# Later modulation columns: multiplied and summed by VectorE, only summed over partitions by TensorE

## The chip, the cores and the metric

The kernel runs on one core of a Trainium2 chip. The metric is device time in microseconds (us) of one launch, the median of several runs. Engines are named as the profile names them: PE (TensorE), DVE (VectorE), ACT (ScalarE), POOL (GpSimd), SP (SyncE, which issues the DMAs here).

## The reference

Two layers of a mixer over 512 latent and 256 context tokens, width 1024, fp32. What matters here is the modulation and where it is used:

```
mod   = silu(c) @ w_mod + b_mod            # 1024 -> 3 x 1024, per layer
mod_c = silu(c_ctx) @ w_mod + b_mod        # the same map for the context tokens
shift, scale, gate = split(mod, 3)
h = rmsnorm(x, norm_w) * (1 + scale) + shift
... three branches from h @ w_in: attention, SSD (Mamba-2), convolution ...
y = g0 * (ua @ w_br_attn) + g1 * (us @ w_br_ssd) + g2 * (uc @ w_br_conv)   # g: sigmoid gates of h
x_new = x + gate * (y @ w_out)             # the last layer keeps only the latent tokens
```

So for each layer 24 blocks of 128 columns (8 shift, 8 scale, 8 gate) are products of a 1024 x 128 weight block with two vectors, silu(c) and silu(c_ctx). Shift and scale are needed at the start of a layer, the gate only in its output projection.

## The kernel before

Activations lie with channels on the 128 partitions and tokens along the row. A projection of 1024 channels is 8 channel tiles deep; each fp32 weight tile is split into a high and a low part (whi by ACT, L156; wlo by DVE, L157), and three products (hi x hi, hi x lo, lo x hi) are summed in one PSUM bank. `wload` (L140) loads a weight tile into one of three `raw` buffers and splits it into five half-tile buffers, at a raised priority (TOP).

The kernel is written in Tile, whose scheduler fixes each engine's order ahead of the run, by priority (program order, less a bonus where the code raises it). From the `man` block (L475) to the end of the attention (L1118) PE's order is as written. There the merges of branch 2 (convolution) and branch 1 (SSD) are woven as small steps between the steps of the SSD scan and of the attention by `Weave` (L190), which paces them by columns (`merge_cols`, L744). The last merge (branch 0, attention; `merge_steps(0, ..., fin=True)`, L1129) and the output projection (`out_tile`, L1147) come after it, and there the scheduler chooses PE's order too.

A merge goes over 8 channel tiles `ct`. Each has a gate (`sig_steps`, 24 products per span of tokens, evacuated by ACT with a tanh) unless that gate is ready in DRAM (`ready`), and the branch product (12 products per span), which DVE evacuates and multiplies with the gate (`br_out`, L718). Both use the PSUM pool `pj`, which has two banks. Layer 0 has spans of 512 and 256 tokens, layer 1 one of 512. In layer 0's last merge tiles 1, 3 and 5 have their gates ready, in layer 1's 1, 3, 5 and 7.

The modulation columns of layer 0 that its start needs (shift and scale, 16 blocks) are made by `mod_tiles` (L221) and don't change. The others, 8 blocks of layer 0 and 24 of layer 1, are made in groups of four blocks, and each group in two halves, `mod_half` (L244): two loads of 512 KB, then 16 matmuls in which a 128 x 32 piece of `sc` (silu(c) and silu(c_ctx) in columns 0 and 1, the rest zero) is the stationary operand and a 128 x 128 weight block moves, on four column groups of PE side by side. ACT copies the first half out of PSUM, DVE adds the second (L262), PE transposes the sum (L266), and DVE adds the bias (L267). One half is a visit. Layer 0's four visits stand in the loop over the convolution projections of the SSD branch (L549); layer 1's twelve stand in layer 0's three merges, one after every second channel tile (L738), and the transposition is put off by MOD_LAG columns of other work (`then`, L674).

Of the kernel before, what the change touches and what calls it, by code (L numbers as in the profile page):

```python
# [15 lines left out]
P = 128  # L16
DM = 1024
KD = DM // P
# [32 lines left out]
MOD_LAG = 12288  # L51
# [6 lines left out]
def hybrid_kernel(ctx, tc, xT, cc, consts, rope, mod_params, params, fnw, w_mod, w_cm, w_q, w_kvd, w_z,  # L58
# [71 lines left out]
    V.memset(nhalf, -0.5)  # L130

# [112 lines left out]
    def mod_half(li, mod, m0, half, part):  # L244


        raws = []
        for i in range(2):
            raw = wp.tile([P, 4, 2, P], F32, tag="raw", name="raw")
            k0 = 4 * half + 2 * i  # L250
            with tc.high_priority(offset=TOP):
                nc.sync.dma_start(raw, w_mod[li, m0:m0 + 4, :, k0:k0 + 2, :].rearrange("m p k c -> p m k c"))
            raws.append(raw)
        ps = pot("ps_mod")
        for i in range(4):
            for j in range(4):
                T.matmul(ps[32 * j:32 * j + 32, 0:P], sc[:, 4 * half + i, :], raws[i // 2][:, j, i % 2, :],
                         start=(i == 0), stop=(i == 3), tile_position=(0, 32 * j))
        if half == 0:
            S.activation(part, ps[:, 0:P], AF.Copy)  # L260
            return None
        V.tensor_tensor(out=part, in0=ps[:, 0:P], in1=part, op=ALU.add)  # L262

        def finish():
            pt = ps[:, P:2 * P]
            T.transpose(pt, part, ident)  # L266
            V.tensor_tensor(  # L267
                out=mod[:, m0:m0 + 4, :], in0=pt.rearrange("p (j r) -> p j r", j=4)[:, :, 0:2],
                in1=pmod[:, li, O_BMOD + m0:O_BMOD + m0 + 4].unsqueeze(2).to_broadcast([P, 4, 2]), op=ALU.add)

        return finish

    class Mods:


        def __init__(self, li, mod, m0):
            self.li, self.mod, self.m0, self.n = li, mod, m0, 0

        def visit(self):
            g, half = divmod(self.n, 2)  # L280
            if half == 0:
                self.part = sm.tile([P, P], F32, tag="part", name="part4")
            self.n += 1
            return mod_half(self.li, self.mod, self.m0 + 4 * g, half, self.part)
# [65 lines left out]
    for li in range(2):  # L350
# [127 lines left out]
        na = sm.tile([P, 16], F32, tag="na", name="na")  # L478
        S.activation(na, par[:, O_AL:O_AL + 16], AF.Exp)
# [52 lines left out]
        gate_mods = Mods(0, mods[0], 16)  # L532
        for ct in range(8):
# [15 lines left out]
            if li == 0 and ct % 2 == 1:  # L549
                fn = gate_mods.visit()  # L550
                if fn is not None:
                    soon.append(fn)
# [121 lines left out]
        def then(fn, steps):  # L674

            done = 0
            for n in steps:
                yield n
                done += n
                if done >= MOD_LAG and fn is not None:  # L680
                    fn()
                    fn = None
            if fn is not None:
                fn()
# [14 lines left out]
        def merge_steps(br, u, first, fin, ready=()):  # L699
# [4 lines left out]
            end = None  # L704
            next_mods = Mods(1, mods[1], 8 * (2, 1, 0)[br])
            for ct in range(KD):
# [15 lines left out]
                if ct in ready:  # L722
                    nc.sync.dma_start(tg, g_dr[ct][:, :ntok])
                else:
                    yield from then(end, sig_steps(br, ct, tg))
                    end = None
                yield from then(end, mm_cm_steps(wb, lambda k: u[0][:, k, :], lambda k: u[1][:, k, :], ntok, br_out,
# [13 lines left out]
            if end is not None:  # L741
                end()
# [556 lines left out]
```

## Time and profile before

| | |
|---|---|
| median of 3 runs | 1493.41 us (1489.54 to 1495.44) |
| the profiled execution | 1494.89 us |
| its span | 1493.1 us |
| mean granted clock of PE | 0.992 of full speed |
| DVE busy | 1037.0 us, 69% |
| ACT busy | 716.4 us, 48% |
| chain that ended last | PE 91%, DVE 2%, ACT 2%, DMA 2% |

A chain's share is the time in which the last instruction's chain of predecessors stood on that engine. An engine's busy time is the union of its instructions; matmuls overlap, so the distance from one start to the next tells more than a matmul's duration. Layer 0's last merge lies from 739 to 812 us, its output stage to 880, layer 1's last merge from 1380 to 1430.

### The profile page before, as it was taken

The numbers are of one execution on the slowest core, as the hardware profiler recorded it, in microseconds if no ns is written. First come the engines' busy times: TensorE is split into PE (matmuls) and PEld (weight loads), VectorE is DVE, ScalarE is ACT, GpSimd is POOL, SyncE is SP. The second block draws the span as 40 slices with busy tenths as digits, with TensorE's granted clock in tenths as the row PEclk, the third lists the DMA queues.
The fourth block names the chain that finished last, engine by engine and source line by source line (L and its number), as shares of the span: only waits on it lengthen the run. The fifth ranks groups of instructions, "written<-read, shape, count | busy, mean of one in ns | idle before, by whom it ended". The sixth has DMA issues, their size and how long they took to land.

```text
span 1493.1 us, 24893 instructions
## 1 busy us (share of the span) xinstructions
PE 1443.5 (97%) x9660; PEld 1252.6 (84%) x9660; DVE 1037.0 (69%) x1895; ACT 716.4 (48%) x1600; POOL 81.7 (5%) x177
## 2 busy tenths in 40 slices
PE   5999999999998999999999999999999999999997
PEld 5889899988887888888888877989988887888886
DVE  4689998665657775555444378999977788666554
ACT  4423543365444476555422254355455547666431
POOL 0000010100001210000000000001010121000000
PEclk9999999999999999999999999999999999999999
DMA  9222343212334323313653532223423342223542
GB/s 376 68 75 94 98 129 111 75 61 99 100 113 135 116 76 129 107 64 121 236 167 105 173 113 87 82 59 114 154 71 108 99 151 80 98 85 99 176 139 81
DMA packets 81975, 172.58 MB, mean 116 GB/s; under 512 B 7872, under 2 KB 40768, under 8 KB 81856
## 3 DMA queue, kind: packets, MB, share of 16 engines
q1 hardware_dynamic: 81856, 170.98, 35.2%
q8 instruction: 76, 1.25, 0.4%
q14 instruction: 43, 0.35, 0.1%
HBM read 143.43 MB, written 27.53 MB: 114 GB/s over the span
## 4 chain that ended last, share of the span: by engine, by line
PE 91%; DVE 2%; ACT 2%; DMA 2%; issue 1%; SPq 0%; POOL 0%; POOLq 0%; DVEq 0%; ACTq 0%
PE ps_gm L175 22%; PE ps_br L175 11%; PE ps_xbc L175 8%; PE ps_o L175 7%; PE ps_gcv L175 4%; PE ps_g L175 4%; PE ps_u L175 3%; PE po_v L1079 3%; PE ps_ga L175 3%; PE pt_p L1065 3%; PE ps_l L1019 2%; PE ps_z L216 1%; PE ps_c L1019 1%; PE ps_q L217 1%; PE ps_q L216 1%; PE ps_z L217 1%
## 5 line engine op out<-in xcount | busy, mean ns | idle before, releaser
L156 ACT ACTIVATE whi<-raw 128x512 fp32r<-128x512 f32 (+1 forms) x316 | 198.9, 632 | 294.7 <-PE ps_gm L175 60.9
L157 DVE TENSOR_TENSOR wlo<-raw,whi 128x512 fp32r<-128x512 f32 (+1 forms) x316 | 216.8, 690 | 150.6 <-ACT whi L156 146.3
L441 DVE SCALAR_TENSOR_TENSOR vacc<-vt,par,vacc 128x783 f32<-128x783 f32 (+1 forms) x232 | 207.0, 892 | 7.9 <-ACT vacc L438 4.2
L175 PE MATMUL ps_gm<-hh,whi 128*128 128x512 f32 (+1 forms) x576 | 212.3, 369 | 0.0
L175 PE MATMUL ps_gm<-hh,wlo 128*128 128x512 f32 (+1 forms) x576 | 209.6, 364 | 0.0
L175 PE MATMUL ps_gm<-hl,whi 128*128 128x512 f32 (+1 forms) x576 | 209.3, 363 | 0.0
L175 PEld LDWEIGHTS ps_gm<-hh,wlo 128*128 128x128 f32 x576 | 109.0, 189 | 15.6 <-issue 2.1
L175 PEld LDWEIGHTS ps_gm<-hh,whi 128*128 128x128 f32 x576 | 109.2, 190 | 15.1 <-issue 2.0
L175 PEld LDWEIGHTS ps_gm<-hl,whi 128*128 128x128 f32 x576 | 109.0, 189 | 14.2 <-issue 1.0
L175 PE MATMUL ps_xbc<-hh,whi 128*128 128x512 f32 (+1 forms) x240 | 82.9, 345 | 0.0
L175 PE MATMUL ps_xbc<-hh,wlo 128*128 128x512 f32 (+1 forms) x240 | 82.1, 342 | 0.0
L175 PE MATMUL ps_xbc<-hl,whi 128*128 128x512 f32 (+1 forms) x240 | 82.0, 342 | 0.0
L175 PE MATMUL ps_o<-yh,whi 128*128 128x256 f32 (+1 forms) x208 | 65.8, 317 | 3.1 <-DVE xnew L1142 3.0
L689 ACT ACTIVATE tg<-ps_gm,hw 128x512 f32<-128x512 f32 x72 | 44.3, 615 | 49.2 <-PE ps_gm L175 48.8
L1071 ACT ACTIVATE pth<-pt_p 128x512 f32<-128x512 f32 x72 | 43.6, 605 | 49.4 <-PE pt_p L1065 49.3
L175 PE MATMUL ps_o<-yl,whi 128*128 128x256 f32 (+1 forms) x208 | 65.7, 316 | 0.0
L175 PE MATMUL ps_o<-yh,wlo 128*128 128x256 f32 (+1 forms) x208 | 65.6, 315 | 0.0
L558 DVE SCALAR_TENSOR_TENSOR xacc<-xraw,par,xacc 128x770 f32<-128x770 f32 (+1 forms) x64 | 62.3, 982 | 2.4 <-ACT xacc L555 2.3
L1025 DVE TENSOR_REDUCE mx<-ps_l 128x1 f32<-128x512 f32 x64 | 44.1, 690 | 26.8 <-PE ps_l L1019 26.1
L1065 PE MATMUL pt_p<-mr,pe 128*128 128x128 f32 x416 | 62.3, 272 | 0.0
L1065 PEld LDWEIGHTS pt_p<-mr,pe 128*128 128x128 f32 x416 | 51.0, 140 | 11.3
L719 DVE SCALAR_TENSOR_TENSOR tg<-tg,ps_br 128x512 f32<-128x512 f32 x66 | 39.6, 600 | 29.1 <-PE ps_br L175 26.2
(281 smaller groups left out, 3641.4 us busy)
## 6 DMA issues: line engine op xcount, KB each, us to landing
raw<-in_w_cm_dram SPq DMA_DIRECT2D x96, 512.0 KB, 3.6
raw<-in_w_mod_dram SPq DMA_DIRECT2D x32, 512.0 KB, 5.0
raw<-in_w_br_dram SPq DMA_DIRECT2D x24, 512.0 KB, 3.6
raw<-in_w_out_dram SPq DMA_DIRECT2D x21, 512.0 KB, 3.7
wm<-in_w_mod_dram SPq DMA_DIRECT2D x16, 512.0 KB, 8.6
ydr<-tg SPq DMA_DIRECT2D x16, 384.0 KB, 3.5
yo<-ydr SPq DMA_DIRECT2D x16, 384.0 KB, 3.5
raw<-in_w_z_dram SPq DMA_DIRECT2D x8, 512.0 KB, 3.9
```

Of the source, the lines that this page charges most:

```text
L156: S.activation(hi, raw[:, u0:u0 + m, :], AF.Copy)
L157: V.tensor_tensor(out=lo, in0=raw[:, u0:u0 + m, :], in1=f(hi), op=ALU.subtract)
L175: T.matmul(ps[:, :b - a], st[:, col], mv(k)[:, a:b], start=(n == 0), stop=(n == len(order) - 1))
L441: V.scalar_tensor_tensor(out=acc[:, :n] if j else vt[:, o:o + n], in0=vt[:, o + j:o + j + n], scalar=cw(j), in1=acc[:, :n], op0=ALU.mult, ...
L558: xm = V.scalar_tensor_tensor(out=acc[:, :n], in0=raw[:, j:j + n], scalar=par[:, O_SCW + ct * 5 + j:O_SCW + ct * 5 + j + 1], in1=acc[:, :n ...
L689: lambda ps, a, b: S.activation(tg[:, a:b], ps, AF.Tanh, scale=0.5, bias=hw[:, br * 8 + ct:br * 8 + ct + 1]), "ps_gm")
L719: V.scalar_tensor_tensor(out=tg[:, a:b], in0=tg[:, a:b], scalar=1.0, in1=ps, op0=ALU.add, op1=ALU.mult)
L1019: T.matmul(ps[:, 0:b - a], qts[g][:, hq + j, tok(qi)], kk[:, i, g, a:b], start=(i == 0), stop=(i == 1))
L1025: V.tensor_reduce(out=mx[:, 0, j:j + 1], in_=pl[j], axis=AX.X, op=ALU.max, negate=True)
L1065: T.transpose(pt[:, tok(2 * i + j)], pes[j][:, tok(k1 + i)], ident)
L1071: S.activation(pf, pt, AF.Copy)
L1079: T.matmul(po[64 * j:64 * j + 64, 0:P], vv[:, k0 + k1 + i, g, :], pth[:, i, j, :], start=(k1 + i == 0), stop=(k1 + i == nk - 1), tile_posi ...
```

## The change

The visits go. `Mods` now holds a list of groups. `feed` loads a quarter of a group (four blocks, two of the eight channel tiles deep, 512 KB) and has DVE multiply it with the two scalars per partition and add it to two accumulators of 128 x 512 (one for c, one for c_ctx), all at the raised priority. `turn` does one of two things: for a group whose four feeds are issued, eight matmuls that sum the accumulators over the partitions, with a constant `pick` as the stationary operand (a column of ones in a 128 x 32 piece, so that row 0 gets c and row 1 c_ctx), and ACT's copy; at the next call that group's transposition and bias. Layer 0's gate columns and layer 1's shift and scale are fed in layer 0's last merge (two feeds per channel tile, 16) and after its first three output tiles (8 more); layer 1's gate columns in layer 1's last merge (8 feeds, in the first four channel tiles). The merges that are woven into the SSD stage and the attention have no modulation work any more, and `merge_cols` no longer counts it. The accumulators come from the pool of small tiles (7 buffers of 128 x 512). `na` is made in place in `par`.

```diff
-MOD_LAG = 12288
...
+    pick = const.tile([P, 33], F32, name="pick")
+    V.memset(pick, 0.0)
+    V.memset(pick[:, 1:2], 1.0)
...
+        def feed(self):
+            g, q = divmod(self.n, 4)
+            if g >= len(self.groups):
+                return
+            self.n += 1
+            li, m0 = self.groups[g]
+            raw = wp.tile([P, 4, 2, P], F32, tag="raw", name="mraw")
             with tc.high_priority(offset=TOP):
+                nc.sync.dma_start(raw, w_mod[li, m0:m0 + 4, :, 2 * q:2 * q + 2, :].rearrange("m p k c -> p m k c"))
+                if q == 0:
+                    self.acc = [small([P, 4, P], F32, "macc") for _ in range(2)]
+                for kk in range(2):
+                    for r in range(2):
+                        acc, c = self.acc[r], sc[:, 2 * q + kk, r:r + 1]
+                        if q == kk == 0:
+                            V.tensor_scalar(out=acc, in0=raw[:, :, kk, :], scalar1=c, scalar2=None, op0=ALU.mult)
+                        else:
+                            V.scalar_tensor_tensor(out=acc, in0=raw[:, :, kk, :], scalar=c, in1=acc, op0=ALU.mult,
+                                                   op1=ALU.add)
+            if q == 3:
+                self.ready.append((li, m0, self.acc))
+
+        def turn(self):
+            if self.last is not None:
...
+                T.transpose(pt, part, ident)
...
+            elif self.ready:
+                li, m0, acc = self.ready.pop(0)
+                ps = pot("ps_mod")
+                for r in range(2):
+                    for j in range(4):
+                        T.matmul(ps[32 * j:32 * j + 32, 0:P], pick[:, 1 - r:33 - r], acc[r][:, j, :], start=(r == 0),
+                                 stop=(r == 1), tile_position=(0, 32 * j))
+                part = sm.tile([P, P], F32, tag="part", name="part4")
+                S.activation(part, ps[:, 0:P], AF.Copy)
+                self.last = li, m0, ps, part
...
-        na = sm.tile([P, 16], F32, tag="na", name="na")
-        S.activation(na, par[:, O_AL:O_AL + 16], AF.Exp)
+        na = par[:, O_AL:O_AL + 16]
+        S.activation(na, na, AF.Exp)
...
-            if li == 0 and ct % 2 == 1:
-                fn = gate_mods.visit()
...
+        md = Mods([(1, 16), (1, 20)] if last else [(0, 16), (0, 20)] + [(1, m0) for m0 in (0, 4, 8, 12)])
...
-                    yield from then(end, sig_steps(br, ct, tg))
+                    yield from sig_steps(br, ct, tg)
...
-                if not last and ct % 2 == 1:
-                    end = next_mods.visit()
-                    yield 2048
...
-        merge_cols = KD * (36 * ntok + (0 if last else 1024))
+                if fin:
+                    if ct >= 2:
+                        md.turn()
+                    md.feed()
+                    md.feed()
+
+        merge_cols = KD * 36 * ntok
...
         run(merge_steps(0, ua, False, True, AHEAD_TILES[:ahead1]))
+        if last:
+            for _ in range(4):
+                md.turn()
...
             for ct in range(OUT_FIRST):
                 out_tile(ct, (lat, cx))
+                md.turn()
+                md.feed()
+                md.feed()
+                md.feed()
             for span in (lat, cx):
                 for ct in range(OUT_FIRST, KD):
                     out_tile(ct, (span,))
+                    md.turn()
```

## Rows read from the trace of the kernel before

**Rows 1.** The page: PE's busy time and share; PE and DVE in 40 slices.
```profile
PE 1443.5 (97%) x9660; PEld 1252.6 (84%) x9660; DVE 1037.0 (69%) x1895; ACT 716.4 (48%) x1600; POOL 81.7 (5%) x177
...
PE   5999999999998999999999999999999999999997
...
DVE  4689998665657775555444378999977788666554
```

**Rows 2.** Busy time by stretch: PE, PEld, DVE, ACT, POOL (x instructions), clock, DMA share, GB/s.
```profile
720.00:740.00 20.00, 19.25 (x116) 15.97 (x117) 8.29 (x15) 7.17 (x11) 0.00 (x0) 1.00 0.74 246
740.00:812.00 72.00, 72.00 (x491) 60.73 (x490) 32.01 (x49) 20.07 (x32) 0.00 (x0) 1.00 0.50 161
812.00:835.00 23.00, 22.86 (x127) 19.65 (x126) 8.82 (x14) 4.64 (x7) 0.00 (x0) 1.00 0.43 138
...
1380.00:1400.00 20.00, 20.00 (x94) 16.15 (x91) 9.93 (x16) 8.48 (x15) 0.00 (x0) 1.00 0.63 204
1400.00:1435.00 35.00, 35.00 (x173) 29.40 (x172) 22.30 (x34) 13.29 (x23) 0.00 (x0) 1.00 0.52 157
```

**Rows 3.** The instructions on ps_mod: count, ns (min/median/max), first and last start, forms.
```profile
L257 PE MATMUL ps_mod<-raw,sc x512: 272/273/297, 142.3 to 787.0; 128*32 128x128 f32 x171
```

**Rows 4.** PE in order of time around one visit: start us, us, instruction.
```profile
142.06 0.28 PE L175 MATMUL ps_xbc<-hh,wlo 128*128 128x256 f32 x1
142.27 1.08 PE L257 MATMUL ps_mod<-raw,sc 128*32 128x128 f32 x32
143.28 0.50 PE L175 MATMUL ps_xbc<-hh,whi 128*128 128x512 f32 x1
143.62 0.40 PE L175 MATMUL ps_xbc<-hl,whi 128*128 128x512 f32 x1
```

**Rows 5.** The chain in order of time, both last merges: start us, us, what.
```profile
747.28 0.57 PE ps_mod L257 x16
...
758.74 0.34 PE ps_mod L257 x2
...
762.58 1.63 PE ps_br L175 x12
...
769.19 8.42 PE ps_gm L175 x48
...
812.88 7.70 PE ps_o L175 x42
...
1396.93 5.51 PE ps_gm L175 x24
```

**Rows 6.** PE's waits over the whole span: total us, times, longest us.
```profile
PE ps_mod L266 <- DVE part L262: 2.3, 2, 1.4
```

**Rows 7.** The instructions on vt, layer 0: the layer norm's transpositions.
```profile
L608 PE MATMUL pt_ln<-mr,vt x24: 270/272/273, 272.4 to 288.9; 128*128 128x128 f32 x24
```

**Rows 8.** DVE in order of time: layer 0's last tap, and layer 1's start.
```profile
267.10 1.04 DVE L441 SCALAR_TENSOR_TENSOR vt<-vt,par,vacc 128x783 f32<-128x783 f32 x1
...
883.96 4.06 DVE L386 SCALAR_TENSOR_TENSOR ht<-xnew,aw,rb 128x512 f32<-128x512 f32 x6 [0.76 <-ACT rb L331]
```

**Rows 9.** DVE's groups by shape: busy us, mean ns of one, idle before.
```profile
L719 DVE SCALAR_TENSOR_TENSOR tg<-tg,ps_br 128x512 f32<-128x512 f32 x45 | 30.8, 685 | 23.0 <-PE ps_br L175 20.2 <-DMA tg<-gdr 2.2
...
L386 DVE SCALAR_TENSOR_TENSOR ht<-xnew,aw,rb 128x512 f32<-128x512 f32 x8 | 5.6, 748 | 0.8 <-ACT rb L331 0.8
...
L846 DVE TENSOR_SCALAR xt<-y,ssr 128x512 f32<-128x512 f32 x10 | 4.9, 485 | 4.2 <-POOL ssr L138 4.2
```

**Rows 10.** The page's DMA issues: count, KB each, median us to landing.
```profile
raw<-in_w_cm_dram SPq DMA_DIRECT2D x96, 512.0 KB, 3.6
raw<-in_w_mod_dram SPq DMA_DIRECT2D x32, 512.0 KB, 5.0
```

**Rows 11.** SP's waits from 690 to 880 us: total us, times, longest us.
```profile
SPq L148 <- DVE wlo L157: 68.5, 17, 12.9
```

More of the change, by code (lines that the diff above doesn't have):

```diff
@@ L242, in mod_tiles @@
         return finish
[L244 to L250, printed above, removed]
-            with tc.high_priority(offset=TOP):
[L252 to L284, printed above, removed]
+    class Mods:
+        def __init__(self, groups):
+            self.groups, self.n, self.ready, self.last = groups, 0, [], None
+        def feed(self):
[5 more added lines that the diff above has]
+            raw = wp.tile([P, 4, 2, P], F32, tag="raw", name="mraw")
+            with tc.high_priority(offset=TOP):
+                nc.sync.dma_start(raw, w_mod[li, m0:m0 + 4, :, 2 * q:2 * q + 2, :].rearrange("m p k c -> p m k c"))
[13 more added lines that the diff above has]
+            if self.last is not None:
+                li, m0, ps, part = self.last
+                self.last = None
+                pt = ps[:, P:2 * P]
+                T.transpose(pt, part, ident)
+                V.tensor_tensor(
+                    out=mods[li][:, m0:m0 + 4, :], in0=pt.rearrange("p (j r) -> p j r", j=4)[:, :, 0:2],
+                    in1=pmod[:, li, O_BMOD + m0:O_BMOD + m0 + 4].unsqueeze(2).to_broadcast([P, 4, 2]), op=ALU.add)
+            elif self.ready:
[8 more added lines that the diff above has]
+                self.last = li, m0, ps, part
@@ L531, in hybrid_kernel @@
         late, soon = [], []
-        gate_mods = Mods(0, mods[0], 16)
         for ct in range(8):
@@ L548, in hybrid_kernel @@
                 late.pop(0)()
-            if li == 0 and ct % 2 == 1:
-                fn = gate_mods.visit()
-                if fn is not None:
-                    soon.append(fn)
             n = XN if nx > NL else NL
@@ L672, in hybrid_kernel @@
         yh, yl = [], []
[L674 to L684, printed above, removed]
+        md = Mods([(1, 16), (1, 20)] if last else [(0, 16), (0, 20)] + [(1, m0) for m0 in (0, 4, 8, 12)])
         def sig_steps(br, ct, tg):
@@ L703, in merge_steps @@
                 yl.extend([yb[:, i, :] for i in range(4)] + [work([P, ntok], F32R, "yl") for _ in range(4)])
-            end = None
-            next_mods = Mods(1, mods[1], 8 * (2, 1, 0)[br])
             for ct in range(KD):
@@ L724, in merge_steps @@
                 else:
-                    yield from then(end, sig_steps(br, ct, tg))
-                    end = None
-                yield from then(end, mm_cm_steps(wb, lambda k: u[0][:, k, :], lambda k: u[1][:, k, :], ntok, br_out,
-                                                 "ps_br", slice(c0, c0 + P)))
-                end = None
+                    yield from sig_steps(br, ct, tg)
+                yield from mm_cm_steps(wb, lambda k: u[0][:, k, :], lambda k: u[1][:, k, :], ntok, br_out,
+                                       "ps_br", slice(c0, c0 + P))
                 if not first:
@@ L737, in merge_steps @@
                     V.scalar_tensor_tensor(out=b, in0=tg, scalar=0.5, in1=f(a), op0=ALU.mult, op1=ALU.subtract)
-                if not last and ct % 2 == 1:
-                    end = next_mods.visit()
-                    yield 2048
-            if end is not None:
-                end()
-        merge_cols = KD * (36 * ntok + (0 if last else 1024))
+                if fin:
[4 more added lines that the diff above has]
+        merge_cols = KD * 36 * ntok
         gate_cols = (4 - GATES_EARLY[li]) * 24 * ntok
```

## The prediction

> **What bounds the kernel now.** I read the page's busy line and its slices first: PE is busy for 97% of the span, nine tenths or more in nearly every slice, while DVE swings between four tenths and nine [rows 1]. Then the chain in order of time: through layer 0's last merge and into the output stage it is made of PE's products, one behind the other [rows 5]. So a microsecond of TensorE work is a microsecond of time almost everywhere. Last the table by stretch, for what DVE has left where the change puts its work: idle are 11.7 us of the 20 ahead of layer 0's last merge, 40 of the 72 in it, 14 of the 23 in which the first three output tiles are made, and 23 of the 55 of layer 1's last merge [rows 2].
>
> **What goes from TensorE.** Sixteen visits of 16 matmuls, which the profile records as 512 [rows 3]; twelve stand ahead of layer 0's last merge, four in it. One visit by itself: between the product ahead of it, at 142.06, and the second one behind it, at 143.62, lie 1.56 us; the 256-column and the 512-column step that also lie there would have made 0.35 (24 of each in 8.42 us [rows 5]). A visit costs 1.20 us, of which the records themselves are 1.01 (142.27 to 143.28) and 0.19 the change into and out of it [rows 4]. Twelve are 14.4 us. In the last merge PE's order isn't written by hand, and the scheduler scattered the four visits in eleven clumps: seven of 14 or 16 records that hold the chain for 0.57 us, four of 2 to 6 that hold it for 0.34 [rows 5]; with 0.19 each that is 7 x 0.76 + 4 x 0.53 = 7.4 us. Twice PE stood at a transposition until DVE had summed the halves, 2.3 us in all [rows 6]; those two transpositions will have other work ahead of them. All eight transpositions stay. Removed: 14.4 + 7.4 + 2.3 = 24.1 us.
>
> **What comes to TensorE.** Eight groups get one pick each: 8 matmuls of the same shape, so 16 records, 0.76 us as a clump. Bounds: 0.53 (the small clumps) and 1.2 (a visit, if it is torn apart). By the row with its number of records 6.1 us: three picks in layer 0's last merge, three in its output stage, two in layer 1's last merge. Net PE work: -18.0 us.
>
> Does the gain arrive? Four of the visits stand in the conv stage of layer 0, 4.8 us. What comes due behind it is the layer norm, whose transpositions start at 272.4 [rows 7]; the last convolution tap on DVE, which they read, ends at 268.1 [rows 8], so 4.2 us pass freely and at most 0.6 us is lost. The other eight are among the woven steps of the SSD stage and the attention, where PE's slices stand at nine [rows 1], and count in full.
>
> **What comes to VectorE.** A feed is four operations on 128x512 in fp32, each with a pointer scalar. The nearest row is ht, also with a pointer scalar and two inputs: 0.75 us for one [rows 9], but six back to back in 4.06 us, so 0.66 from start to start [rows 8]; the two accumulators alternate, so neighbours don't depend on each other either. Two of a group's sixteen only multiply, 0.49 us in the row of that shape [rows 9], some 0.40 back to back. A feed is 2.65 us, a group 14 x 0.66 + 2 x 0.40 = 10.1; layer 0's 24 feeds are 61 us, layer 1's 8 are 20. If each operation took its full duration it would be 0.75 and 69 us; I take 0.66, by the row of the same shape in a row of its own kind.
>
> The Trainium skill, "VectorE: DVE Perf Modes", "The DRAIN you can't avoid", speaks against the change here: it has the next operation start only once the pipe of the one before is empty, by which a feed would be 3.0 us. The six in 4.06 us don't agree with that.
>
> The 61 us must find room: idle from 720 to 835 are 66 us [rows 2], and the first group's loads can pass ahead of that. So it fits, but DVE comes to nine tenths in a stretch where it was at 44%. I expect a cost in three places.
> - Evacuations. Feeds run at the highest priority, br_out (0.69 us for 512 columns [rows 9]) at the ordinary one. The pool pj has two banks: after the first 512 columns of a channel tile PE fills the other with 256, 1.63 us [rows 5], and then needs the first one back. One feed in front of br_out delays it by 2.65 at most, 1.0 more than that cover; two by 5.3, 3.7 more. There are eight such evacuations in layer 0, so the bounds are 0 and 29 us. A feed's tile takes 5.0 us to land against 2.65 of work on it [rows 10], so two in a row should be the exception: I take 3.
> - The three raw slots. A feed holds one for 5.0 + 2.65 = 7.7 us; a weight tile for 3.6 us of landing [rows 10] and two splits, some 6.2. The first three output tiles need 8 of the one and 3 of the other: 80 us of slot over 3 slots are 27, where PE needs 23 (7.7 a tile [rows 5]). But the weights were early: 17 times SP waited for a slot behind wlo, 68.5 us in all [rows 11]. Bounds 0 and 4; I take 2.
> - Layer 1's last merge, which had no such work. Its 20 us of feeds are issued within the first two pairs of channel tiles, and a pair takes PE 11 us (24 products in 5.51 us for the gate, as many for the two branches [rows 5]). The first group can pass during the attention; the second stands ahead of the ua splits and of four evacuations, each with 2.8 us of cover (12 products): 0 to 10 us. I take 2.
>
> The accumulators also take buffers of the small pool (7), from which xr is loaded early now; a tile's 7.7 us of PE work hides a later load. If that cover went, an output tile would wait some 4 us, the landing of a weight tile as the nearest transfer, and for one of them at most; I count nothing. The pick constant and the exponential in place are a few short operations beside the first loads, with PE waiting for DMA: nothing, and under 1 us without that cover.
>
> **The sum.** -24.1 + 6.1 + 3 + 2 + 2 = -11.0 us. It is made against the profiled execution's 1494.9 us (span 1493.1), which is 1.5 above the median of the three runs, 1493.4. Against that median: 1482 us. About 0.5%, 7.5 us, is what a measurement of this kernel can tell from no change: faster is below 1485.9, slower above 1500.9.
>
> **The rivals.**
> 1. All vector work hides: -18.0 us, 1475. For it: DVE's idle time there is above the feeds' sum, and around 950 us PE's slices stay at nine beside DVE's at nine [rows 1]. Against it: in those slices DVE's bulk is convolution taps, which give way; the feeds don't.
> 2. The delays eat most of the gain: 16 us in place of 7 (four of the eight evacuations behind two feeds are 15 already), 1491, no change. For it: the weights share slots and priority with the feeds. Against it: SP's waits behind wlo show loads that are ahead of their use.
> 3. Slower: DVE becomes the bound of layer 0's last merge. Two feeds stand ahead of each of the eight first evacuations: 8 x 3.7 = 29 us, less 18: 1505. It decides from five of the eight (5 x 3.7 = 18.5). For it: a slot that comes free is filled at once, so while PE computes on a ready tile (24 products, half of a gate's 8.42 us [rows 5]) feeds can pile up landed, and they go first. Against it: a feed works 2.65 us and lands in 5.0, so DVE empties the slots faster than one slot fills.
>
> By the rule of the emptied pipe two feeds would be 6.0 us and the third rival 35 - 18 = 17 us slower, 1510.
>
> **How the numbers follow.** The forecast has 0.45, the first rival 0.15, the second 0.18, the third 0.22. The forecast's own range, 1477 to 1487, has its upper tenth within 0.5%. Faster 0.15 + 0.9 x 0.45 = 0.55; same 0.18 + 0.05 = 0.23; slower 0.22. The range takes in all but the far part of the third rival: 1475 to 1502.
>
> **What would show it.** Right: the layer norm's first transposition near 268 (four visits earlier), the attention's end some 16 us earlier, and no wait of ps_mod for part; the products on mraw at 0.66 us from start to start; DVE at nine tenths in layer 0's last merge; and in PE's waits a new line, ps_gm or ps_br behind DVE's tg, with 3 to 7 us. Wrong: that line above 18 us (slower); feeds at 0.75 or more; or an attention that ends no earlier, which would mean that PE wasn't what set those stages.

## The result, and the profile after

The kernel after takes 1506.3 us (median of 4 runs, 1503.29 to 1510.89) against 1493.0 us before (4 runs): a ratio of 1.0083, 95% interval 1.0057 to 1.011. It is slower by 0.8%, where 0.7% faster was forecast, and above the top of the range. A profile is one execution, and those of one kernel differ by several us: the profiled one of after is the fastest of its four, 1503.3 us with a span of 1501.5, so the trace shows 8.4 us of the 13.

PE's busy time fell by 4 us and DVE's rose by 77; the chain, which was 91% PE, is now 82% PE. The page of after: the busy line, the chain, and the new products (x count | busy us, mean ns | idle before).

```profile
PE 1439.7 (96%) x9276; PEld 1244.0 (83%) x9276; DVE 1114.0 (74%) x2017; ACT 714.0 (48%) x1600; POOL 86.3 (6%) x177
...
PE 82%; DVE 5%; DMA 5%; ACT 4%; issue 2%; SPq 0%; POOLq 0%; DVEq 0%; POOL 0%; ACTq 0%
...
L273 DVE SCALAR_TENSOR_TENSOR macc<-mraw,sc,macc 128x512 f32<-128x512 f32 x112 | 79.0, 745 | 3.3 <-DMA mraw<-in_w_mod_dram 3.1
```

The stretches of [rows 2] in after (columns as there):

```profile
720.00:740.00 20.00, 17.80 (x109) 14.48 (x109) 16.63 (x27) 5.96 (x10) 0.00 (x0) 1.00 0.76 258
740.00:812.00 72.00, 70.01 (x426) 59.41 (x428) 63.42 (x103) 19.26 (x32) 0.00 (x0) 0.98 0.64 205
812.00:835.00 23.00, 20.96 (x125) 17.13 (x125) 15.38 (x28) 3.85 (x7) 0.00 (x0) 0.93 0.69 234
1380.00:1400.00 20.00, 18.15 (x78) 12.98 (x77) 16.68 (x28) 6.89 (x12) 0.00 (x0) 0.84 0.77 262
1400.00:1435.00 35.00, 32.42 (x152) 25.34 (x151) 27.42 (x44) 11.93 (x21) 0.00 (x0) 0.99 0.65 202
```

PE had no gap in the row from 740 to 812 and now has 2 us; DVE went from 32 to 63 of 72 us; the DMA engines from 0.50 to 0.64, and the clock is below 1 in four rows. The next table has the stages of one profile for each kernel, in us, cut at the last end of po_v (attention), the first start of ps_o (output stage) and its last end. The first two columns are points in time (LN is layer 0's layer norm, the first pt_ln), the others lengths; the kernels below "after" are those of the experiments.

| kernel, one profile each | LN starts at | attention ends at | layer 0's last merge | its output stage | on to the end of layer 1's attention | layer 1's last merge | span |
|---|---|---|---|---|---|---|---|
| before | 272.4 | 716.3 | 96.4 | 68.6 | 499.2 | 49.6 | 1493.1 |
| after | 269.4 | 703.7 | 100.8 | 75.2 | 499.8 | 60.1 | 1501.5 |
| neither loads nor products | 269.0 | 703.9 | 93.5 | 71.0 | 504.1 | 51.7 | 1486.1 |
| products late, no loads | 269.5 | 705.1 | 92.3 | 73.2 | 497.9 | 57.2 | 1487.9 |
| products late, loads unread | 269.6 | 704.3 | 93.9 | 74.3 | 500.8 | 61.8 | 1497.2 |
| products early, no loads | 270.2 | 704.8 | 112.2 | 68.8 | 498.4 | 63.1 | 1509.2 |
| small tiles, layer 1 by PE | 271.2 | 706.5 | 98.7 | 71.9 | 497.4 | 49.6 | 1485.4 |

After is 12.6 us ahead when layer 0's attention ends, loses 11.0 of that in layer 0's last merge and output stage, and 10.5 more in layer 1's last merge. The stretch on to the end of layer 1's attention holds no work that the change moves, and yet it is between 497 and 504 us in the profiles; so a difference of a few us between two totals can lie there. PE's waits for DVE's evacuations, from 690 to 885 (us in total, times, longest), are new; before had two rows of 0.9 us in that window, neither of this kind.

```profile
PE ps_gm L177 <- DVE tgr L715: 2.3, 2, 2.0
...
PE ps_o L177 <- DVE xnew L1139: 2.0, 1, 2.0
PE ps_gm L177 <- DVE tg L715: 1.7, 1, 1.7
PE ps_br L177 <- DVE tg L715: 1.5, 1, 1.5
```

These waits are 7.5 us, and the two longest cost more than their length. The chain through those two (start us, us, what), and the windows around the first (columns as in [rows 2]):

```profile
756.41 1.41 DVE macc L273 x2
758.47 10.25 PE ps_gm L177 x48
...
816.37 10.25 PE ps_o L177 x48
...
826.97 8.62 PE ps_o L177 x48
```

```profile
756.40:758.40 2.00, 0.08 (x1) 0.00 (x0) 2.00 (x5) 0.84 (x1) 0.00 (x0) 1.00 0.82 237
758.80:762.10 3.30, 3.30 (x9) 2.59 (x8) 3.30 (x6) 0.00 (x0) 0.00 (x0) 0.50 0.77 243
762.30:768.70 6.40, 6.40 (x42) 5.60 (x42) 4.92 (x7) 2.75 (x5) 0.00 (x0) 1.00 0.72 224
```

Two products stand on DVE ahead of the evacuation (tgr), PE is idle for 2 us, and the clock granted next is 0.50, 1.2 GHz in place of 2.4. The same 48 products that took 8.42 us [rows 5] take 10.25, so this wait costs another 1.8. The 48 behind the second wait take 10.25 us too, and the next 48 of the same kind 8.62. In layer 1's last merge the chain is off PE from 1384.9 to 1414.4. Its two largest pieces are transfers, with the first products of a feed behind them:

```profile
1386.02 6.36 DMA og<-odr
1392.94 5.17 DMA mraw<-in_w_mod_dram
1398.13 0.88 DVE macc L271 x2
```

On SP, from 690 to 885, the 68.5 us that weight loads waited for wlo, for a slot [rows 11], have become waits of both kinds of loads for both kinds of readers (L264 is the feed's load, L150 a weight's):

```profile
SPq L264 <- DVE macc L273: 27.7, 13, 3.6
SPq L150 <- DVE wlo L159: 26.3, 13, 3.5
SPq L264 <- DVE wlo L159: 22.6, 7, 12.6
SPq L150 <- DVE macc L273: 20.4, 9, 4.0
```

### The profile page after: what moved, and what is told of

It is laid out like the page before. It is cut to its first block, busy times and chain, and to the rows that moved or that the text cites. A ratio compares the mean times of both kernels' runs of the same rounds, so it can differ in the third digit from the quotient of the medians.

```text
span 1501.5 us, 24261 instructions
## 1 busy us (share of the span) xinstructions
PE 1439.7 (96%) x9276; PEld 1244.0 (83%) x9276; DVE 1114.0 (74%) x2017; ACT 714.0 (48%) x1600; POOL 86.3 (6%) x177
## 4 chain that ended last, share of the span: by engine, by line
PE 82%; DVE 5%; DMA 5%; ACT 4%; issue 2%; SPq 0%; POOLq 0%; DVEq 0%; POOL 0%; ACTq 0%
PE ps_gm L177 19%; PE ps_br L177 9%; PE ps_xbc L177 8%; PE ps_o L177 6%; PE ps_u L177 4%; PE ps_gcv L177 4%; PE ps_g L177 4%; PE po_v L1073 3%; PE pt_p L1059 3%; PE ps_ga L177 2%; DMA mraw<-in_w_mod_dram 2%; PE ps_l L1013 2%; DVE macc L273 2%; PE ps_c L1013 1%; PE ps_q L219 1%
## 5 line engine op out<-in xcount | busy, mean ns | idle before, releaser
L273 DVE SCALAR_TENSOR_TENSOR macc<-mraw,sc,macc 128x512 f32<-128x512 f32 x112 | 79.0, 745 | 3.3 <-DMA mraw<-in_w_mod_dram 3.1
```

The lines of the kernel that those rows point to most:

```text
L273: V.scalar_tensor_tensor(out=acc, in0=raw[:, :, kk, :], scalar=c, in1=acc, op0=ALU.mult, op1=ALU.add)
```

## The experiments

Times are medians; the kernel before, run beside each, stood at 1493.5 to 1494.4, and each ratio is against it, with its 95% interval. The intervals are 3 to 9 us wide, so a difference of 2 or 3 us between two experiments isn't clear of the noise. The theories: the products on DVE delay what PE waits for; the feeds' loads delay the weights and tiles that PE waits for; or the removal from PE was never worth 18 us.

### Taking the change apart: neither, the one, the other

**Neither.** No loads, and products on 4 of 512 columns. In this run, and in the others below whose products read something else than their weights, the picks' copy is also scaled by 1e-6.

```diff
-            raw = wp.tile([P, 4, 2, P], F32, tag="raw", name="mraw")
+            raw = src.rearrange("p (m c) -> p m c", m=4)   # a tile of yh, or xnew in the output stage
...
-                            V.scalar_tensor_tensor(out=acc, in0=raw[:, :, kk, :], scalar=c, in1=acc, op0=ALU.mult,
+                            V.scalar_tensor_tensor(out=acc[:, :, 0:1], in0=raw[:, :, 0:1], scalar=c, in1=acc[:, :, 0:1], op0=ALU.mult,
```

> As the kernel without the feeds' loads, and with all but the first two products of a group on 4 of 512 columns: neither loads nor DVE work of size are left, only the picks. Both theories: what the removal from PE is worth by itself, 1476 to 1484 us. If it is above 1490, the removed visits were not worth their PE time, and neither loads nor products explain the loss.

1487.6 us, ratio 0.9955 (0.9938 to 0.9972). With nearly all of the added work gone but the picks, the removal is worth 7 us, not 18.

**Products, no loads.** The first line of that edit alone; the products have their full size, and come when the merge has made the tile that they read.

> The feeds' 32 loads are left out; their products work on the tile that the channel tile has just made (yh, xnew), so the modulation values are wrong (and scaled down). DVE does the same 128 operations on 128x512 at nearly the same places. Theory D (DVE's work is what delays the evacuations): the waits for tg stay, 1498 to 1506 us. Theory L (the loads' landing and their raw slots are what is late): 1482 to 1490.

1492.3 us, 0.9987 (0.9975 to 0.9998): the products in this place add 4.8. They don't add it at layer 0's evacuations: PE's waits for tg and tgr are 1.2 us (690 to 885). In layer 1's last merge, which is 5.5 us longer than with neither, PE waits 3.7 us at two picks for products that come late (1340 to 1445).

```profile
PE ps_br L177 <- DVE tg L714: 0.6, 1, 0.6
PE ps_gm L177 <- DVE tgr L714: 0.6, 1, 0.6
```

```profile
PE ps_mod L292 <- DVE macc L272: 3.7, 2, 1.8
```

**Loads, hardly any products.** The second part of that edit alone; products on 4 of 512 columns of what was loaded.

> All but the first two products of each group work on 4 of the 512 columns, so the modulation values are wrong; loads, order of issue, picks and the number of DVE instructions stay. Theory E (feeds stand ahead of br_out and xnew on DVE, PE waits, its clock drops after the wait): DVE loses 112 x 0.5 = 56 us, PE's waits for tg and xnew go, 1480 to 1485 us. Theory L (the feeds' 512 KB loads take raw slots and DMA time from weights and og): the loads are all still there, so the last merges stay long, 1497 or more.

1500.0 us, 1.0036 (1.0023 to 1.005): the loads add 12.5 to the kernel with neither. DVE now stands in front of loads that haven't landed, with tg and tgr queued behind. DVE's waits and PE's, 700 to 885:

```profile
DVE macc L273 <- DMA mraw<-in_w_mod_dram: 24.2, 15, 3.5
...
DVE macc L271 <- DMA mraw<-in_w_mod_dram: 15.1, 6, 3.4
```

```profile
PE ps_gm L177 <- DVE tgr L715: 3.9, 3, 2.1
...
PE ps_br L177 <- DVE tg L715: 2.1, 2, 1.3
PE ps_o L177 <- DVE tg L715: 1.6, 1, 1.6
```

With a wait of 0.6 these are 8.2 us for evacuations, more than the 5.5 in the change, with hardly any vector work in the feeds; layer 0's last merge takes 103.1 us. Shortly before each of PE's four longest of these waits DVE had stood idle for a load, for 1.5 to 3.5 us. DVE ahead of the last one (idle time and its end in brackets):

```profile
807.93 0.49 DVE L273 SCALAR_TENSOR_TENSOR macc<-mraw,sc,macc 128x4 f32<-128x4 f32 x2 [2.92 <-DMA mraw<-in_w_mod_dram]
...
808.73 0.68 DVE L715 SCALAR_TENSOR_TENSOR tg<-tg,ps_br 128x512 f32<-128x512 f32 x1
```

So from neither to both there are 18.7 us; the loads are the larger part, and the term that I had at 2 us.

### How the loads cost

**A quarter of the bytes**, the same slots and products (which read one block four times).

```diff
-                nc.sync.dma_start(raw, w_mod[li, m0:m0 + 4, :, 2 * q:2 * q + 2, :].rearrange("m p k c -> p m k c"))
+                nc.sync.dma_start(raw[:, 0:1, :, :], w_mod[li, m0:m0 + 1, :, 2 * q:2 * q + 2, :].rearrange("m p k c -> p m k c"))
...
-                            V.scalar_tensor_tensor(out=acc, in0=raw[:, :, kk, :], scalar=c, in1=acc, op0=ALU.mult,
+                            V.scalar_tensor_tensor(out=acc, in0=raw[:, 0:1, kk, :].to_broadcast([P, 4, P]), scalar=c, in1=acc, op0=ALU.mult,
```

> Each feed loads one of the four 128-column blocks (a quarter of the bytes) into the same raw slot, and the products read that block four times over; the sums are therefore not those of the reference. Operations, slots and the order on the queue stay. Left alone, the loads cost 14.0 us (1506.3 with both, 1492.3 with the products and no loads). If what costs is the bytes (the DMA engines are 66% busy in layer 0's last merge, and weights and og land later), three quarters of it go: about 1496. If what costs is that a feed holds one of three raw slots from its issue to its last product, the landing shrinks from 3.5 us to perhaps 2.5 and the hold from about 6.2 to 5.2: 1503 to 1505. If it is only the place in SP's queue, the time stays at 1506.

1498.9 us, 1.0034 (1.0016 to 1.0052): 7.4 of the 14 come back. A load lands in 2.1 us in place of 3.8 (700 to 835), so a slot's hold and DVE's wait for a load are shorter too; bytes, hold and that wait aren't told apart by this run.

**Tiles of the small pool** in place of raw slots.

```diff
-            raw = wp.tile([P, 4, 2, P], F32, tag="raw", name="mraw")
+            raws = [small([P, 4, P], F32, "mraw") for _ in range(2)]
...
+                for kk in range(2):
+                    nc.sync.dma_start(raws[kk], w_mod[li, m0:m0 + 4, :, 2 * q + kk, :].rearrange("m p c -> p m c"))
```

> Each feed loads its two 128x512 blocks into two tiles of the small pool (seven buffers, two of them accumulators) in place of one raw slot: the raw slots belong to the weights alone, as in the kernel without loads, while bytes and products stay; there are twice as many transfers on SP. If the slots cost the 14 us: 1492 to 1497. If it is the bytes or the queue: 1505 or more. The small pool also holds tiles of the attention and of the output stage, which can wait then: that would show as DVE or ACT waits at those tiles.

1503.2 us, 1.0052 (1.0036 to 1.0069): 3 us less than the change, not clear of the noise. Each load is now two of 256 KB. In its profile layer 0's two stages are 7.5 us shorter than after's, while layer 1's last merge is 3.6 longer.

**Both**: the small tiles of this edit, and in each the one block of the edit before.

> Loads of a quarter of the bytes (the products read one 128-column block four times over, so the sums are not the reference's) into tiles of the small pool: bytes and raw slots both relieved. If bytes and slots add up, 1506.3 - 7.4 - 3.1 = 1495.8. If the one only works through the other (a large transfer holds a slot longer), relieving both gives little more than the bytes alone: 1498 to 1499. If together they release what either alone holds back, it comes to the kernel without loads: 1492 to 1494; then bytes and slots are the whole of the 14 us.

1498.4 us, 1.0042 (1.0028 to 1.0056): no more than the quarter loads alone. It is still 6 us above the kernel without loads, with a quarter of the bytes left and none of the raw slots; so the raw slots aren't all of the loads' cost.

**Issued by GpSimd.**

```diff
-                nc.sync.dma_start(raw, w_mod[li, m0:m0 + 4, :, 2 * q:2 * q + 2, :].rearrange("m p k c -> p m k c"))
+                nc.gpsimd.dma_start(raw, w_mod[li, m0:m0 + 4, :, 2 * q:2 * q + 2, :].rearrange("m p k c -> p m k c"))
```

> The feeds' loads are issued by GpSimd in place of SyncE; slots, bytes and products stay. If the loads cost by standing in SP's queue, where a load that waits for a slot holds back the weights and og behind it, most of the 14 us go: 1493 to 1497. If it is the slots or the bytes, 1504 to 1508. If GpSimd issues a transfer slowly, or its own work holds the loads back, it is later: above 1508.

1504.6 us, 1.0064 (1.0047 to 1.0081). Taking the feeds' loads off SP's queue gave 1.7 us, not clear of the noise. The slots are still shared: a weight's load waits 28.0 us, ten times, for a product to give one back (690 to 885). The feeds' loads land in 4.8 us in place of 3.5 here, so a gain in the queue could be hidden by that.

**Loads that nobody reads**, products late and from other tiles.

```diff
+            load = wp.tile([P, 4, 2, P], F32, tag="raw", name="mraw")
             raw = src.rearrange("p (m c) -> p m c", m=4)
             with tc.high_priority(offset=TOP):
+                nc.sync.dma_start(load, w_mod[li, m0:m0 + 4, :, 2 * q:2 * q + 2, :].rearrange("m p k c -> p m k c"))
```

> As the run without loads (products read tiles that the merge makes; 1492.3), but every feed also issues its 512 KB load into a raw slot, and nothing reads it; the sums are not the reference's. If the loads cost by themselves (bytes, slots, SP's queue), 1499 or more. If they cost only because VectorE's products follow them, the time stays at 1492 to 1494.

1501.1 us, 1.0041 (1.0023 to 1.006): 8.8 above the same kernel without loads. No instruction reads these loads; they take slots, SP's queue and the DMA engines. The chain at the start of layer 1's last merge is made of them, one behind the other, and of the gate tile behind them:

```profile
1376.97 6.22 DMA mraw<-in_w_mod_dram
1383.21 4.55 DMA mraw<-in_w_mod_dram
1387.79 5.92 DMA mraw<-in_w_mod_dram
1394.45 5.98 DMA tg<-gdr
```

The four tiles tg landed in 2.6 us at the median before, here in 3.3. Layer 0's last merge, by contrast, is hardly longer than without loads (93.9 us against 92.3), and PE's waits for tg and tgr are 1.0 us. In the kernel with neither, the chain of layer 1's stretch is PE's products alone:

```profile
1375.91 7.42 PE ps_gm L177 x32
...
1394.36 5.61 PE ps_br L177 x24
```

**Products that are ready at once**, no loads.

```diff
-                    md.feed(f(a)[:, 0:512])
+                    md.feed(f(u[0][:, 0, 0:512]))       # the branch's input; yh[0] in the output stage
```

> As the run without loads, but the products of the merges read the branch's input, which is there from the merge's start, and those of the output stage a tile that the merge has finished: they are ready at once, at the highest priority, and no load paces them; the sums are not the reference's. If about 6 us of the loads' 14 are the products' early place, ahead of tg, ua and wlo on VectorE: 1498 or more, with PE waiting for tg and ua. If the place is worth nothing, 1492 to 1494, and the 6 us belong to the transfers as such.

1512.6 us, 1.0121 (1.0093 to 1.0149): 20 us above the same products in the late place. At the start of layer 0's last merge this is the pile-up of the third rival. DVE in order of time (start us, us), and what PE waits for (690 to 885):

```profile
730.61 5.39 DVE L272 SCALAR_TENSOR_TENSOR macc<-ua,sc,macc 128x512 f32<-128x512 f32 x8
735.91 1.02 DVE L714 SCALAR_TENSOR_TENSOR tg<-tg,ps_br 128x512 f32<-128x512 f32 x2
736.84 4.74 DVE L272 SCALAR_TENSOR_TENSOR macc<-ua,sc,macc 128x512 f32<-128x512 f32 x7
741.48 0.97 DVE L724 TENSOR_TENSOR tg<-tg,yo 128x768 f32<-128x768 f32 x1
742.34 4.74 DVE L272 SCALAR_TENSOR_TENSOR macc<-ua,sc,macc 128x512 f32<-128x512 f32 x7
746.98 0.71 DVE L714 SCALAR_TENSOR_TENSOR tgr<-tgr,ps_br 128x512 f32<-128x512 f32 x1
```

```profile
PE ps_gm L177 <- DVE tgr L714: 5.3, 1, 5.3
PE ps_br L177 <- DVE tg L714: 4.7, 2, 4.5
```

Seven or eight products pass ahead of the first two evacuations, later ones have one to three, and layer 0's last merge takes 112.2 us (the output stage's products pass up into it as well). In the change two products stood ahead of the evacuations that PE waited for, and PE waited 2 us at most. So the loads cost, and by pacing the products they also keep them from doing worse.

### Is it the order?

Evacuations above the feeds (br_out of both last merges, xnew of layer 0); products at the ordinary priority; products and loads at the ordinary priority.

```diff
+                    with tc.high_priority(offset=2 * TOP) if fin else nullcontext():
                         V.scalar_tensor_tensor(out=tg[:, a:b], in0=tg[:, a:b], scalar=1.0, in1=ps, op0=ALU.add,
```

> br_out of the last merges and layer 0's xnew get a priority above the feeds. Theory E: PE's waits for tg, tgr and xnew (10 us in the profile after, and the half clock behind two of them) go, 1490 to 1496 us. Theory O (DVE is simply full in those stretches, whoever goes first): the waits pass to wlo, ua or the picks and the time stays within 3 us of 1506. Theory L: stays at 1506.

> The feeds' VectorE operations at the ordinary priority of the merge's own work, their loads at the highest as before. If the products' place ahead of tg, ua and the splits is what the loads add beyond their 8 to 9 us, it comes to the run with unread loads: about 1501. If the loads carry the whole, 1505 to 1507. A product that waits longer also holds its raw slot longer: that would be above 1507.

> Products and loads at the ordinary priority, so that a weight tile's load and split go ahead of a feed. If it is the order in which loads and products are issued that costs, 1495 to 1500; if it is the bytes and the slots whatever their order, 1501 to 1507.

1504.0 us (1.007, 1.0047 to 1.0094), 1504.2 (1.0072, 1.005 to 1.0095) and 1504.5 (1.0076, 1.0057 to 1.0095): all three within after's interval. With the evacuations first PE still waits 2.7 us for tgr and 3.1 for tg, and in the two others 5.1 to 5.5 us for both. Rank alone, in any of these forms, doesn't repair it.

### Where the work stands

**Visits of PE at the new places**, no vector products (one visit per channel tile in the last merge, one after each output tile).

```diff
-                    if ct >= 2:
-                        md.turn()
-                    md.feed()
-                    md.feed()
+                    md.visit()
```

> The visits of the kernel before, on PE, at the places where the change has its feeds: eight in layer 0's last merge, four in its output stage, four in layer 1's last merge; no products on DVE. Same loads at nearly the same places as after. Theory E and O: no wait for tg, PE work as before the change, 1490 to 1496 us. Theory L: the loads still crowd the last merges, 1500 us or more.

1517.3 us, 1.0149 (1.012 to 1.0179), slower than the change: PE now reads the raw tiles itself and holds their slots until it gets to them, and weights come late (two of PE's waits, 700 to 1445):

```profile
PE ps_gm L177 <- ACT whi L158: 4.7, 2, 3.2
PE ps_mod L259 <- DMA raw<-in_w_mod_dram: 2.5, 3, 1.1
```

With loads into raw slots, the last merges and the output stage are a bad place for this work on PE too. (For layer 0 that changes with the tiles that the loads go to, as the faster version below shows.)

**Feeds in the woven merges**: one or two per channel tile in layer 0's woven merges and one in its last, or two per channel tile in the two woven ones only.

```diff
-                if fin:
-                    if ct >= 2:
-                        md.turn()
-                    md.feed()
-                    md.feed()
+                md.turn()
+                for _ in range(1 if fin else 1 + ct % 2):     # or: range(0 if fin else 2)
+                    md.feed()
```

> The same feeds and picks, all 32 in layer 0, spread over its three merges: three per two channel tiles in the woven merges of branches 2 and 1, one per channel tile in the last merge, none in the output stage and none in layer 1. Loads and DVE work fall where DVE is 60% busy and DMA 30%. Both theories: the last merges get short again, 1480 to 1488 us, faster than before the change; if the small pool's buffers (two per group, shared with SSD and attention) are what costs, 1495 or more.

> The same feeds, two per channel tile in the two woven merges of layer 0, none later. Layer 0's last merge has then neither visits nor feeds: 66 us in place of 73.7 before and 78.9 after. 1478 to 1488 us by both theories, unless DVE's work delays the SSD steps and the attention's transpositions, which PE then shows as waits for DVE there.

1527.9 us (1.0228, 1.021 to 1.0246) and 1517.8 (1.0148, 1.0127 to 1.017). The last merges are at 50 us (layer 1) and below 93 (layer 0) again, but the SSD stage and the attention pay more: in the first of the two the attention ends at 753.8 us, 50 later than in after. Whether the products or the small pool's buffers hold these stages up isn't told. PE waits for DVE's own steps in them (300 to 720):

```profile
PE pseg L793 <- DVE al L790: 12.7, 11, 3.7
PE pt_p L1057 <- DVE pe L1043: 8.9, 3, 4.5
```

**Layer 1's gate columns by PE**, four visits in the woven merge of branch 2 in layer 0; the six other groups as in the change.

```diff
-        md = Mods([(1, 16), (1, 20)] if last else [(0, 16), (0, 20)] + [(1, m0) for m0 in (0, 4, 8, 12)])
+        md = Mods([] if last else [(0, 16), (0, 20)] + [(1, m0) for m0 in (0, 4, 8, 12)])
...
+                if not last and br == 2 and ct % 2 == 1:
+                    end = next_mods.visit()
+                    yield 2048
```

> Layer 1's two gate groups are made as before the change, four visits in layer 0's woven merge of branch 2; all else as after. All theories that put the loss at the feeds: layer 1's last merge goes back from 49.6 to 39 us, four visits cost 4.8 us, so 1506 - 10.6 + 4.8 = 1500 us. If that merge stays above 45 us, what lengthened it is not the feeds in it.

1497.7 us, 1.0027 (1.0014 to 1.0041): 8.6 us less than the change, which is 13 above before. Layer 1's last merge is back at 49.5 us.

### A version that is faster than both

**Small tiles, and layer 1's gate columns by PE.**

> The small tiles of the run before, and layer 1's two gate groups by visits of TensorE in the middle merge of layer 0 (which took 1506.3 to 1497.7 when done alone). If the raw slots are what the loads cost, the two together come to 1486 to 1491, below the kernel before; if they are not, 1497 to 1500.

1488.9 us, 0.9955 (0.9938 to 0.9971). It beats the kernel before by 5 us, clear of the interval, and the change by 17. Its row for the start of layer 1's last merge, to set beside the fourth of [rows 2]:

```profile
1380.00:1400.00 20.00, 20.00 (x88) 16.26 (x87) 11.78 (x18) 8.53 (x15) 0.00 (x0) 1.00 0.68 218
```

PE is busy throughout at the full clock. Small tiles were worth 3.1 us in the change and 8.8 here. In the change, layer 1's last merge lost again about half of what they gave in layer 0. But not all of the 8.8 is theirs: between the two profiles with layer 1's gate columns by PE, 4.8 us lie in layer 0's two stages and 6.5 in the stretch behind, which the edit doesn't touch.

**The same with the products at the ordinary priority.**

> The version with small tiles and layer 1's gate groups by TensorE (1488.9), with the products at ordinary priority. If the products' place still costs there, 1483 to 1487; if small tiles have already paced them well enough, 1488 to 1490; if they come late for their groups' picks, above 1491.

1489.9 us, 0.9975 (0.9963 to 0.9987): no better, in line with the order experiments.

## Why the prediction was wrong

Two terms of the sum were mis-sized: the gain by 11 us, and the raw slots, the only term for the loads, by 7 to 12.

| step | predicted, us | measured, us | by |
|---|---|---|---|
| net work gone from PE, and that it arrives | -18.0 | -6.9 | the kernel with neither, less before |
| products: evacuations 3, layer 1's last merge 2 | 5 | 4.8, at other places | products without loads, less neither |
| loads: the raw slots | 2 (0 to 4) | 8.8 unread, 12.5 with small products, 13.9 in the change | unread less none; small products less neither; the change less products without loads |
| the whole | -11.0 | +13.2 | medians |

It took both. With the loads at 13.9 and the gain as forecast, the sum would be near zero (-18.0 + 4.8 + 13.9); with the gain at 6.9 and the loads as forecast, too (-6.9 + 5 + 2).

**"Does the gain arrive?"** The conv stage was to give 4.2 to 4.8 us. In the profile with neither, 1.6 comes between the first ps_xbc and the layer norm, which starts at 269.0 in place of 268; another 1.8 lies ahead of the first ps_xbc, where there were no visits. The layer norm's own inputs weren't the next thing late. Inside the stage PE now waits longer for ACT, by 3.0 us (140 to 205, before and then after; with neither the same):

```profile
PE pt_x L528 <- ACT bc L564: 1.0, 1, 1.0
```

```profile
PE pt_x L541 <- ACT bc L572: 2.5, 1, 2.5
PE ps_xbc L177 <- ACT xraw L554: 1.5, 2, 0.7
```

The visits had been standing where PE would have waited for ACT; I had looked only at what comes behind the stage, not inside it.

The woven visits were right. Seven of the eight, and one wait of 1.4 us at a transposition, lie between the layer norm's start and the attention's end: 9.8 us, of which 9.0 came. The eighth stands behind the attention's end, at 718.78, with the other wait, 0.9. With these two, four visits less three picks were to give 7.2 us from there to the output stage. Summed from start to next start, the records on ps_mod took 7.7 us there before, 0.9 of it the wait, and 2.8 in the kernel with neither: 4.9. The 0.19 us that I added to each of eleven clumps for the change into and out of it, read off one lone visit, isn't there for a clump. Waits for tgr took 1.7 of the 4.9. The output stage got 2.4 us longer, as three picks of 0.76 should.

Another 4.9 us went between layer 0's end and the end of layer 1's attention in that profile. The change doesn't have them (499.8 us), but four other variants do (503.5 to 504.0). About half of it are longer waits for ACT at ps_u and pt_x, 2.2 us; and the granted clock stands at 0.50 for 10.2 us there in place of 6.8, which is worth 1.7. What sets these off I can't tell; no run ties them to the removed work.

**"The three raw slots."** This is the term that was furthest off. I reckoned slot time against PE's time for three output tiles only and took SP's 68.5 us behind wlo as reserve [rows 11]. But 16 of the feeds' loads fall into the last merge, which has its own weights, og, yo and tgr to fetch, and 8 into layer 1's last merge, which I didn't reckon at all. The reserve was used up: SP's waits behind wlo for a weight fell from 68.5 to 26.3 us, and 20.4 behind macc came up. (The hold itself was, if anything, overestimated: the feeds' tiles landed in 3.5 us at the median, not in the 5.0 that I took.) And I priced only the slots. Loads that nobody reads cost 8.8 us, by slots, queue and bytes together, and with a quarter of the bytes 7.4 us come back. What I left out altogether is that a product whose load is late holds up whatever stands behind it in DVE's order. PE's waits for tg and tgr, and layer 0's last merge, in us:

| | waits, 690 to 885 | layer 0's last merge |
|---|---|---|
| neither loads nor products | 1.7 | 93.5 |
| products late, no loads | 1.2 | 92.3 |
| products late, loads unread | 1.0 | 93.9 |
| loads, hardly any products | 8.2 | 103.1 |
| the change | 5.5 | 100.8 |

So in layer 0's last merge it is neither DVE's work nor the loads by themselves, but products that stand behind their loads.

**Layer 1's last merge.** I took 2 of 0 to 10 us. It is 10.5 longer. About half comes without loads (5.5, above), much of it at picks that wait for late products, which I had not reckoned. For the rest, the start of that stage, from 1380, already had DMA at 0.63 [rows 2]; with 8 loads at the highest priority ahead of og and tg it is at 0.77, and the chain runs through og and a feed's load. I counted DVE's time ahead of ua and left out the transfers that ua comes from.

**Evacuations.** That the products' total, 4.8, meets the 5 us of the sum is luck: without loads the waits for tg and tgr are 1.2 us, and the cost is in the output stage (73.2 us against 71.0) and in layer 1's last merge. In the change the waits are there, 5.5 us, the longer ones of 1.5 to 2.0 us each, more than the 1.0 beyond the cover that I had for one feed; but they come with the loads. I also left out that such a wait can be followed by products at half the clock.

**Durations** were right. The products take 745 ns and stand 0.67 us apart (eight in 5.39 us in the run with early products, two in 1.41 in the change). The Trainium skill, "VectorE: DVE Perf Modes", "The DRAIN you can't avoid", has the next operation start only when the pipe is empty, but adds that one which is not held starts earlier. The prediction left out that second half, and these rows agree with it.

**The rivals.** The third named 1505 us, next to the measured time, but by a mechanism that the change shows only in small: it needs eight products ahead of each first evacuation, and only products without loads that are ready early come near that (112.2 us for the merge). Against it I had said that DVE empties slots faster than one fills. That held. That the measured time lies next to this rival's is luck: it was reached by the loads and the missing gain instead.

**The signs.** What I had named as showing a right forecast nearly all came: the layer norm at 269.4, the attention's end 12.6 us earlier, DVE at 63 of 72 us, and 5.5 us for tg and tgr. None of these signs looked at the loads, the output stage or layer 1's last merge, where the time went.

**What stays open.** Loads unread and products late make 1501.1; in the change, with each product behind its own load, it is 1506.3. The profiles put these 5 us in layer 0's last merge, by the table above; but no edit changed DVE's order alone and took the waits away, so that is read and not shown. Nor is it told how the loads' 8.8 us divide between bytes, SP's queue and the time that a slot is held, since fewer bytes shorten the hold.

## What to carry to other kernels

Price a moved transfer by what the receiving stage already fetches, in each stage that receives it, not by its landing time or the free buffers alone: here 16 MB of loads that nobody reads cost 9 us in stages whose DMA share was 0.4 to 0.7. Before counting work removed from the bounding engine as gained, look inside the stage for waits which that work was covering. When work goes to an engine with slack, ask what stands behind it there while its input is still on the way. And check how early its inputs are ready: unpaced and first in order, the same vector work cost 20 us more than in a later place.

## What the runs showed of the hardware

A PE wait of about 2 us in busy work can be followed by a lower clock, but need not be. In after the granted clock is 0.50 behind the waits of 1.99 us (758.47) and 2.04 us (816.37), and from 1394 to 1400 behind a wait of 1.3. Behind the wait of 2.5 us at pt_x, which ends at 190.16, it stays at 1.00. With the evacuations first, PE waits 2.3 us at the place of the first one, and the 48 products behind it keep the full clock: 8.68 us in place of 10.25. I had priced waits at their length. The window behind pt_x in after, and these products in the chain with the evacuations first:

```profile
190.20:193.60 3.40, 3.40 (x18) 2.94 (x19) 3.40 (x5) 1.17 (x4) 0.00 (x0) 1.00 0.45 147
```

```profile
760.22 8.68 PE ps_gm L177 x48
```

The stretch from layer 0's end to the end of layer 1's attention shows the price over the 20 profiles. It is 497.4 to 498.4 us in the four where the clock stands at 0.50 for 3.4 us of it, 499.0 to 499.9 in the six with 6.8 us, and 500.7 to 504.1 in the ten with 10.2 or more.
